# Both halves' delta rule in one software pipeline, and the samples' state update in two-head steps beside the output tiles

## The chip, the cores and the metric

The kernel runs on one core of a Trainium2 chip. The metric is the device time of one execution in microseconds; a kernel's time is the median of several executions.

## The reference, cut to what matters

The reference is one inference step of a two-layer decoder trunk for a prompt of 2048 tokens and 8 single-token samples, width 1024, all in float32. The change lies in the second (odd) layer:

```python
h = rmsnorm(x, norm_w)
q, k, v, u_sg, v_sg, b, a, gate = split(h @ w_in)      # 768, 768, 768, 256, 256, 6, 6, 1024 columns
q, k, v = split(silu(causal_conv4(concat(q, k, v))))   # 2304 channels
q = l2norm(q) * 128 ** -0.5 ; k = l2norm(k)            # 6 heads of 128
beta = sigmoid(b) ; logg = -exp(a_log) * softplus(a + dt_bias)
c_out = rmsnorm(gated_delta_rule(q, k, v, beta, logg, state))   # per token: S = exp(logg) S + k (beta (v - S'k))'
d_out = gelu(u_sg) * chunk_spatial_gate(rmsnorm(gelu(v_sg)))    # 128-token chunks, lower triangular
y = x + (concat(c_out, d_out) * silu(gate)) @ w_out
```

Outputs are `y` for prompt and samples, the new convolution rows and the new matrix states `S` (128 x 128 per head) of the prompt and of each of the 8 samples (`new_delta_sample`, 8 x 6 x 128 x 128).

## The kernel before, in words

**Matrix products.** Float32 products are made from two parts of each factor (`hi`, `lo`), three matmuls per product (`mm3`, L201 to L203). `fm_block` makes 128 output channels for a block of tokens (24 matmuls). Each 512 KB weight unit is loaded into the tile `wraw` (one buffer in this layer: `self.wbufs[2]` is 1), split by ScalarE (`whi`, L177) and VectorE or GpSimd (`wlo`, L179).

**Halves.** The prompt goes through the layer in two halves of 1024 tokens. For each half `odd` runs: 18 channel blocks `conv_silu` (three pieces of 342 or 340 tokens each; blocks 0 to 5 are q, 6 to 11 k, 12 to 17 v; the result goes to DRAM, `y1`); before block number `CB` = 14 the product for `v_sg`, `b`, `a` (`gated_v`, 8 or 9 token tiles) and the decays (`decay`); then `spatial` (6 pieces) and 24 gate pieces (`gate_block`, 8 units of three). After both halves come 17 output tiles (`out_tile`), the first four of them in two column halves. The output weights are loaded and split beside the first of these (`w_out`, L889 to L892).

**The delta rule** of a half is 16 items: 8 chunks of 128 tokens times two groups of three heads. Its stages are `delta_load` (q, k and decays from DRAM), `delta_front` (transposes and k k', k q' products), `delta_blocks` (VectorE solves 16 x 16 blocks, L1422 and L1424, with two round trips through DRAM), `delta_merge16` (loads v, L1447) and `delta_merge` (the inverse in 32, 64 and 128 wide blocks), `delta_step` (the recurrence through `S`; v is transposed in L1521) and `delta_out`. `blocks`, `merge16` and `merge` work on a pair of items. The table `DORD` gives each stage a lag of 0 to 6 items.

**Side work.** `delta`, `sample_delta` and `w_out` are Python generators in `self.sides`. A call `self.tick(n, kind)` writes the next n pieces of one of them at that place of the program; the delta rule's pieces are written at a high priority (`PRIO`). The final order on each engine is set when the program is built, by a scheduler that weighs the written order, the priorities and its own estimate of durations. On the chip every engine runs its own queue in that order and waits at each instruction until its inputs are there. All DMAs are issued by the SP queue.

**Where the delta rule's pieces stand.** After each half's convolution `self.tick(10000)` finishes the generator of the half before, and a new one is made. The first half's pieces then stand in that half's spatial part and gates and in the second half's convolution, one after each piece (`self.pace` is 1); the second half's in its spatial part, its gates and the output tiles. Output tile t of the second half is written once `self.ndone` items are finished.

**The samples' state.** `sample_delta` runs beside the second half's spatial part and gates. Its first part normalizes the samples' q and k (`rstd` in L125 and L126 on GpSimd), a second part multiplies each of the 8 states with k and q (L1629), and a third updates the states in 16 steps of three heads: load the state (L1649) and a broadcast correction row (L1650, from the DRAM tile `sdd`), three ScalarE multiplications (L1660), three VectorE multiply-adds (L1661), store (L1662). Its buffers are tiles `hx` of the pool `hp` (three buffers, one of them held by the samples' small tiles).

Of the kernel before, what the change touches and what calls it, by code (L numbers as in the profile page):

```python
# [10 lines left out]
F32 = mybir.dt.float32  # L11
# [4 lines left out]
ALU = mybir.AluOpType  # L16
# [4 lines left out]
P = 128  # L21
D = 1024
NT = 2048
NS = 8
NH = 6
# [3 lines left out]
HALF = 1024  # L29
# [7 lines left out]


T0, T1, T2 = 4, 2, 3
VA, VB, CB = 2, 5, 14  # L40
VS, SA = "P", 2
TS = 12
PC = 1
# [20 lines left out]
class Net:  # L64
# [1027 lines left out]
    def odd(self):  # L1092
        nc, I, O = self.nc, self.I, self.O
        st = ExitStack()
        self.banks = dict(OD, h=OD["acc"])
        self.odd_consts(st)
        wk = self.pool(st, "wk", 2)
        hp = self.hp
        dr = self.dram
        self.sg1 = dr.tile([D, NT + NS], F32, name="sg1")  # L1100
        self.cat1 = dr.tile([D, NT + NS], F32, name="cat1")
        self.vd = dr.tile([NT, 256], F32, name="vd")
        self.y1 = dr.tile([2304, NT], F32, name="y1")
        W = I["w_in_o"]
        for half in range(2):
            subs = self.subs if half == 0 else self.load_half(hp, wk)
            self.wsplit = WC if half else WB

            gates = [(W[i], P) for i in range(20, 28)]
            if half == 0:  # L1110
                We = I["w_out_e"]
                mix = [(We[i * 512:i * 512 + 512, cb * 256:cb * 256 + 256].rearrange("(k p) c -> p k c", p=P), 256)
                       for cb in range(4) for i in range(2)]
                gates = [u for g in range(6) for u in (gates[g], mix[g])] + mix[6:] + gates[6:]
            self.nxt = nxt = self.stream([(W[i], P) for i in range(CB)] + [(I["w_vba"][i], 268) for i in range(2)]
                                         + [(W[i], P) for i in range(CB, 20)] + gates, 1)
            for cb in range(18):
                if cb == CB:
                    ba = self.gated_v(half, subs, wk, hp)
                    gt = self.decay(half, ba, wk)  # L1120
                self.conv_silu(half, cb, nxt(), wk)
            if half:
                nc.sync.dma_start(O["new_conv_prompt"].rearrange("(k p) j -> p k j", p=P), self.clast,
                                  allow_slow_non_contiguous=True)
            if half == 0:
                self.tick(10000, "values")
                self.svst.close()
                dl = self.pool(st, "dl", 1, side="right")
            self.tick(10000)
            self.sides["delta"] = self.delta(half, gt, dl)  # L1130
            if half == 1:
                self.sides["sample"] = self.sample_delta(wk, hp)
            self.spatial(half, subs, wk, hp)
            if half == 1:
                self.sample_sg(wk)
            else:
                self.sides["sample"] = self.sample_out(wk, hp)
                self.tick(1, "sample")
            for g in range(6):
                unit = nxt()  # L1140
                for sub in subs:
                    self.gate_block(wk, g, unit, sub)
                    self.tick(half * SA, "sample")
                self.tick(1 - half, "sample")
            self.tick(2 * (1 - half), "sample")
            units = [nxt(), nxt()]
            for sub in subs:
                for g in range(2):
                    self.gate_block(wk, 6 + g, units[g], sub)
                    self.tick(half, "sample")  # L1150
        self.tick(10000, "sample")
        tiles = [tuple(a[:, :, c0:c0 + w] for a in (self.hh, self.hl)) for c0, w in QSUB]
        self.sides["w_out"] = self.w_out(I["w_out_o"], tiles, lambda: hp.tile([P, 4 + HALF], F32, tag="hx", name="wraw"), W2)

        def get(nm):
            if nm in ("whi", "wlo"):
                return self.wp.tile([P, D], F32R, tag=nm, name=nm, bufs=2)
            if nm[0] == "m":
                return self.t512(wk, nm)
            return hp.tile([P, 4 + HALF], F32, tag="hx", name=nm)[:, :D]  # L1160

        def out(t, *grps):
            n, t0 = (P, t * P) if t < 16 else (NS, NT)
            dst = O["y_prompt"][t0:t0 + n] if t < 16 else O["y_sample"]
            self.out_tile(t0, n, self.cat1, self.sg1, get, self.x1[t0:t0 + n], dst, grps)

        self.tick(4, "w_out")
        for t in range(T0):
            out(t, 0)
            self.tick(T1)  # L1170
            self.tick(2, "w_out")
        self.tick(10000, "w_out")
        for t in (*range(TS), 16, *range(TS, 16)):

            while 8 <= t < 16 and self.ndone < 2 * (t - 7):
                self.tick()
            out(t, *((1,) if t < T0 else (0, 1)))
            self.tick(T1 if t < T0 else T2)
        self.tick(10000)
        for g in range(2):  # L1180
            nc.sync.dma_start(O["new_delta_prompt"][g * 3:g * 3 + 3].rearrange("h k v -> k h v"), self.S[g])
        st.close()
# [61 lines left out]
    def conv_silu(self, half, cb, unit, wk):  # L1244

        nc = self.nc
        w = (self.convw, self.convh)[half][:, cb, :]
        for a, n in CSUB:
# [4 lines left out]
            x = self.t512(wk, "cx")[:, :n]  # L1253
# [11 lines left out]
                nc.scalar.activation(th, x, AF.Tanh)  # L1265
                nc.vector.scalar_tensor_tensor(th, th, 1.0, x, ALU.add, ALU.mult)
            self.store(self.y1[cb * P:cb * P + P, half * HALF + a:half * HALF + a + n], th)
            self.tick(self.pace)
            self.tick(1 if a else 2, "values")

    def t512(self, pool, name):
# [23 lines left out]
        nc.sync.dma_start(gd.rearrange("t h i -> (t h) i"), gr)  # L1295
        return beta, nG, kd, gd

    def delta(self, half, gt, dl):

        self.ndone = 0  # L1300
        pairs = [dict(half=half, t=t) for t in range(8)]
        items = [dict(half=half, t=t, g=g, pair=pairs[t]) for t in range(8) for g in range(2)]
        stages = dict(load=self.delta_load, front=self.delta_front, blocks=self.delta_blocks, merge16=self.delta_merge16,
                      merge=self.delta_merge, step=self.delta_step, out=self.delta_out)
        for i in range(len(items) + 6):

            for j, lag in DORD:
                if 0 <= i - lag < len(items):
                    x = items[i - lag]
                    pair = j in ("blocks", "merge16", "merge")  # L1310
                    if not pair or x["g"]:
                        stages[j](x["pair"] if pair else x, gt, dl)
                        if j != "load":
                            yield

# [247 lines left out]
    def sample_delta(self, wk, hp):  # L1563

        nc, I, O = self.nc, self.I, self.O
# [12 lines left out]
        x, tp = f("sx", [P, 18, NS]), f("stp", [P, 18, NS])  # L1578
# [17 lines left out]
        q, k, v = (x[:, i * 6:i * 6 + 6, :].rearrange("p h b -> p (h b)") for i in range(3))  # L1596
# [7 lines left out]
        bb = f("sbb", [P, 2, 48])  # L1604
# [12 lines left out]
        sd = I["state_delta"]  # L1617
# [5 lines left out]
        nx = load(0)  # L1623
# [18 lines left out]
        nc.tensor.transpose(pd[:48, :], dlt, self.ident)  # L1642
        dr = f("sdr", [48, P])
        nc.vector.tensor_copy(dr, pd[:48, :])
        dd = self.dram.tile([NH, NS, P], F32, name="sdd")
        nc.sync.dma_start(dd.rearrange("h b v -> (h b) v"), dr)
        def load2(b, g):
            s = hp.tile([P, 4 + HALF], F32, tag="hx", name="s1")[:, :768].rearrange("p (h v) -> p h v", v=P)
            nc.sync.dma_start(s[:, :3], sd[0, b, g:g + 3].rearrange("h k v -> k h v"))  # L1649
            nc.sync.dma_start(s[:, 3:], dd[g:g + 3, b:b + 1, :].rearrange("h o v -> o h v").broadcast_to([P, 3, P]))  # L1650
            return s[:, :3], s[:, 3:], b, g

        steps = [(b, g) for b in range(NS) for g in (0, 3)]
        nx = load2(*steps.pop(0))
        while nx:
            (s, db, b, g), nx = nx, load2(*steps.pop(0)) if steps else None
            yield
            for h in range(3):
                j = (g + h) * NS + b
                nc.scalar.mul(s[:, h, :], s[:, h, :], bb[:, 1, j:j + 1])  # L1660
                nc.vector.scalar_tensor_tensor(s[:, h, :], db[:, h, :], k[:, j:j + 1], s[:, h, :], ALU.mult, ALU.add)  # L1661
            nc.sync.dma_start(O["new_delta_sample"][b, g:g + 3].rearrange("h k v -> k h v"), s)  # L1662

        nc.vector.tensor_tensor(qkp, o, o, ALU.mult)
        yield
        pr = self.bank("side", P)
        mm(pr[:, :48], self.ones, qkp, start=True, stop=True)
        nc.vector.tensor_scalar(qkp, pr[:, :48], 1.0 / P, None, ALU.mult)
# [1 line left out]
        nc.vector.tensor_tensor(o, o, qkp, ALU.mult)  # L1670
        nc.vector.tensor_scalar(o, o, self.onw, None, ALU.mult)
        nc.sync.dma_start(self.cat1[:768, NT:].rearrange("(h p) b -> p h b", p=P), o.rearrange("p (h b) -> p h b", b=NS))

    def sample_sg(self, wk):
        nc, I, O = self.nc, self.I, self.O
# [123 lines left out]
```

## Time and profile before

| | us |
|---|---|
| three executions, median (lowest to highest) | 3059.98 (3048.13 to 3065.13) |
| profiled execution, its own time | 3062.73 |
| its span, first to last instruction | 3060.6 |

| engine | busy us | share |
|---|---|---|
| TensorE (PE) | 2788.8 | 91% |
| its weight loads (PEld) | 2535.1 | 83% |
| VectorE (DVE) | 2087.6 | 68% |
| GpSimd (POOL) | 1654.7 | 54% |
| ScalarE (ACT) | 1375.1 | 45% |

Busy shares are averages over stages with different limits; the odd layer's second half is the part from about 2095 us on. `PEclk` is the granted TensorE clock as a share of full speed (2.4 GHz); the two levels are 1.0 and 0.5, so 0.86 over a stretch means that 28% of it ran at 1.2 GHz. An idle time is put down to the event that ended it.

### The profile page before, as it was taken

Reading aid. Unit: us, or ns where it says so; the run is one execution under the profiler, and the core shown is the slowest. Engines: PE = TensorE matmul, PEld = TensorE weight load, DVE = VectorE, ACT = ScalarE, POOL = GpSimd, SP = SyncE. Lnnn points to the kernel's source line nnn. Section 1 sums busy time; section 2 is a strip of 40 time slices with the busy share of each in tenths; the row PEclk is TensorE's granted clock in tenths of the full one; section 3 lists DMA queues with packets and bytes.
Section 4 is the critical chain, followed back from the end, with each engine's and each line's share of the span. In section 5 each row is a group of like instructions: output and inputs, shape, how many; then the busy total and the mean of one; then the engine's idle time right before and its main releaser. Section 6 shows DMA issues by size and latency. Waiting matters only on the chain. (4 is left out here: it accounts for less than half of the span.)

```text
span 3060.6 us, 57584 instructions
## 1 busy us (share of the span) xinstructions
PE 2788.8 (91%) x20425; PEld 2535.1 (83%) x20425; DVE 2087.6 (68%) x4067; ACT 1375.1 (45%) x3995; POOL 1654.7 (54%) x1249
## 2 busy tenths in 40 slices
PE   8998999999998899989888989999999879788999
PEld 8998999989777777769778878878899868677887
DVE  5465466563998899875677877568877574556652
ACT  5323332224877787762223233445554533444331
POOL 5666546550666876665675655454544253256541
PEclk9999999999999999999999999999999989989999
DMA  6779988868234413227776655444333234467543
GB/s 233 255 242 317 319 280 297 257 198 238 58 90 118 124 56 91 73 79 218 237 239 202 195 178 166 133 128 126 104 94 97 87 83 117 131 190 209 147 113 100
DMA packets 440154, 506.57 MB, mean 166 GB/s; under 512 B 86331, under 2 KB 339684, under 8 KB 439868
## 3 DMA queue, kind: packets, MB, share of 16 engines
q1 hardware_dynamic: 439868, 502.90, 54.0%
q8 instruction: 162, 2.65, 0.4%
q14 instruction: 124, 1.02, 0.1%
HBM read 347.09 MB, written 155.69 MB: 164 GB/s over the span
## 5 line engine op out<-in xcount | busy, mean ns | idle before, releaser
L201 PE MATMUL acc<-bh,whi 128*128 128x256 f32 (+4 forms) x1208 | 406.2, 336 | 15.9 <-ACT whi L910 6.7
L202 PE MATMUL acc<-bl,whi 128*128 128x256 f32 (+4 forms) x1208 | 404.4, 335 | 0.9 <-DVE bl L892 0.9
L203 PE MATMUL acc<-bh,wlo 128*128 128x256 f32 (+4 forms) x1208 | 402.6, 334 | 2.7 <-DVE wlo L911 1.8
L855 POOL TENSOR_TENSOR p<-p,cf 128x512 f32<-128x512 f32 (+3 forms) x240 | 236.8, 1005 | 218.6 <-DVE cf L839 69.8
L832 ACT ACTIVATE p<-sc,nb 128x512 f32<-128x512 f32 (+3 forms) x480 | 302.2, 642 | 73.4 <-DVE nb L831 59.8
L645 POOL TENSOR_TENSOR kp<-kp,at 128x768 f32<-128x768 f32 x120 | 201.4, 1687 | 173.2 <-DMA kp<-in_cache_v 152.2
L203 PE MATMUL cv<-bh,wlo 128*128 128x346 f32 (+2 forms) x864 | 284.3, 330 | 6.4 <-DVE wlo L179 4.4
L831 DVE TENSOR_REDUCE nb<-sc 128x1 f32<-128x512 f32 (+3 forms) x480 | 276.1, 598 | 18.7 <-PE sc L830 9.4
L201 PE MATMUL cv<-bh,whi 128*128 128x346 f32 (+2 forms) x864 | 284.8, 330 | 2.9 <-DVE vv L1036 1.8
L202 PE MATMUL cv<-bl,whi 128*128 128x346 f32 (+2 forms) x864 | 284.5, 329 | 0.0
L567 POOL TENSOR_TENSOR kp<-kp,qb 128x768 f32<-128x768 f32 x88 | 166.2, 1894 | 191.0 <-DMA kp<-in_cache_k 145.2
L201 PEld LDWEIGHTS acc<-bh,whi 128*128 128x128 f32 (+1 forms) x1208 | 232.7, 193 | 32.6 <-ACT whi L910 7.6
L201 PE MATMUL acc<-whi,bh 128*128 128x256 f32 x864 | 247.8, 287 | 7.6 <-ACT whi L177 6.0
L202 PE MATMUL acc<-wlo,bh 128*128 128x256 f32 x864 | 247.1, 286 | 2.7 <-POOL wlo L179 1.9
L203 PEld LDWEIGHTS acc<-bh,wlo 128*128 128x128 f32 (+1 forms) x1208 | 232.4, 192 | 19.5 <-DVE wlo L911 2.9
L203 PE MATMUL acc<-whi,bl 128*128 128x256 f32 x864 | 246.5, 286 | 0.0
L202 PEld LDWEIGHTS acc<-bl,whi 128*128 128x128 f32 (+1 forms) x1208 | 232.6, 193 | 15.2 <-DVE bl L892 1.3
L647 DVE TENSOR_TENSOR sacc<-sacc,kp 128x768 f32<-128x768 f32 x120 | 184.2, 1535 | 78.7 <-POOL kp L645 68.6
L827 PE MATMUL sc<-kh,q 128*128 128x512 f32 (+2 forms) x480 | 210.5, 439 | 25.3 <-ACT p L832 22.0
L869 PE MATMUL pv<-v,pt 128*128 128x128 f32 x1632 | 219.1, 282 | 15.2 <-ACT pt L867 8.5
L869 PEld LDWEIGHTS pv<-v,pt 128*128 128x128 f32 x1632 | 202.6, 195 | 29.8 <-ACT junk L872 13.6
L179 POOL TENSOR_TENSOR wlo<-wraw,whi 128x1024 fp32r<-128x1024 f32 (+1 forms) x62 | 151.7, 2449 | 89.2 <-ACT whi L177 77.7
(445 smaller groups left out, 8339.8 us busy)
## 6 DMA issues: line engine op xcount, KB each, us to landing
kp<-in_cache_k SPq DMA_DIRECT2D x128, 384.0 KB
kp<-in_cache_v SPq DMA_DIRECT2D x128, 384.0 KB
wraw<-in_w_in_o SPq DMA_DIRECT2D x56, 512.0 KB
mc<-cat SPq DMA_DIRECT2D x72, 256.0 KB
mg<-sg SPq DMA_DIRECT2D x72, 256.0 KB
wraw<-in_w_in_e SPq DMA_DIRECT2D x28, 512.0 KB
wsplit<-whi SPq DMA_DIRECT2D x28, 512.0 KB
wsplit<-wlo SPq DMA_DIRECT2D x28, 512.0 KB
```

The lines of the kernel that those rows point to most:

```text
L179: e.tensor_tensor(lo, raw, hi.bitcast(F32), ALU.subtract)
L201: mm(out, ah, bh, start=first, stop=False)
L202: mm(out, ah, bl, start=False, stop=False)
L203: mm(out, al, bh, start=False, stop=last)
L567: (nc.vector if j % 3 == 2 else nc.gpsimd).tensor_tensor(k, k, qb, ALU.mult)
L645: nc.gpsimd.tensor_tensor(h3(w), h3(v), self.at[:, b, j, :, None].broadcast_to([P, NH, P]), ALU.mult)
L647: nc.vector.tensor_tensor(acc, acc, v, ALU.add)
L827: mm(sc[:, :w], qc, kh[:, c, :w], start=True, stop=False)
L831: nc.vector.tensor_reduce(nb[:, c, j:j + 1], sc[:, :n], AX.X, ALU.max, negate=True)
L832: nc.scalar.activation(p[:, c, :n], sc[:, :n], AF.Exp, bias=nb[:, c, j:j + 1], accum_out=l[:, c, j:j + 1])
L855: nc.gpsimd.tensor_tensor(p[:, 1, :n], p[:, 1, :n], cf[:, 1, j:j + 1].broadcast_to([P, n]), ALU.mult)
L869: mm(pv, tt[:, t, :], kvt[j][2][:, t, :], start=j == 0 and t == 0, stop=j * 4 + t == nk - 1)
```

## The change

The two delta generators become one over 32 items. Items of the second half may load q and k once `self.ready` is 1 (from channel block 12 on), and load v and go into `merge16` once it is 2 (after the second half's convolution); until then the generator gives its turn away. The first half's pieces are no longer finished by `tick(10000)`. In the second half `gated_v` and `decay` move from before channel block 14 to before block 10, and a convolution block gets two pieces of the delta rule, not three. The samples' state update leaves `sample_delta`; it becomes a generator of its own, `sample_state`, with 24 steps of two heads, whose two buffers lie in one tile of `wraw`. It is written from the output weights on, one or two steps per output tile. Two small tiles (`skg`) keep the samples' k and decay for it.

```diff
-VA, VB, CB = 2, 5, 14
+VA, VB, CB = 2, 5, (14, 10)
@@ odd
+        self.ndone, self.gts, self.ready = 0, [], 0
         for half in range(2):
...
             for cb in range(18):
-                if cb == CB:
+                if cb == CB[half]:
                     ba = self.gated_v(half, subs, wk, hp)
-                    gt = self.decay(half, ba, wk)
+                    self.gts.append(self.decay(half, ba, wk))
+                if half and cb == 12:
+                    self.ready = 1
                 self.conv_silu(half, cb, nxt(), wk)
...
-                dl = self.pool(st, "dl", 1, side="right")
-            self.tick(10000)
-            self.sides["delta"] = self.delta(half, gt, dl)
+                self.sides["delta"] = self.delta(self.pool(st, "dl", 1, side="right"))
+            else:
+                self.ready = 2
             if half == 1:
+                self.sdd = dr.tile([NH, NS, P], F32, name="sdd")
+                self.skg = wk.tile([P, 2, NH * NS], F32, name="skg", bufs=1)
                 self.sides["sample"] = self.sample_delta(wk, hp)
...
         self.tick(10000, "sample")
+        self.sides["state"] = self.sample_state()
...
         for t in range(T0):
             out(t, 0)
             self.tick(T1)
+            self.tick(1, "state")
             self.tick(2, "w_out")
...
-            while 8 <= t < 16 and self.ndone < 2 * (t - 7):
+            while 8 <= t < 16 and self.ndone < 2 * (t + 1):
                 self.tick()
             out(t, *((1,) if t < T0 else (0, 1)))
             self.tick(T1 if t < T0 else T2)
+            self.tick(1 if t < T0 else 2, "state")
         self.tick(10000)
+        self.tick(10000, "state")
@@ conv_silu
-            self.tick(self.pace)
+            self.tick(self.pace if a else 0)
@@ delta
-        self.ndone = 0
-        pairs = [dict(half=half, t=t) for t in range(8)]
-        items = [dict(half=half, t=t, g=g, pair=pairs[t]) for t in range(8) for g in range(2)]
+        pairs = [dict(half=half, t=t) for half in range(2) for t in range(8)]
+        items = [dict(half=y["half"], t=y["t"], g=g, pair=y) for y in pairs for g in range(2)]
...
-                        stages[j](x["pair"] if pair else x, gt, dl)
+                        while x["half"] and self.ready < dict(load=1, merge16=2).get(j, 0):
+                            yield
+                        stages[j](x["pair"] if pair else x, self.gts[x["half"]], dl)
@@ sample_delta
...
+        nc.sync.dma_start(self.sdd.rearrange("h b v -> (h b) v"), dr)
+        nc.vector.tensor_copy(self.skg[:, 0, :], k)
+        nc.vector.tensor_copy(self.skg[:, 1, :], bb[:, 1, :])
+    def sample_state(self):
+        nc, sd, out = self.nc, self.I["state_delta"], self.O["new_delta_sample"]
+        buf = self.wp.tile([P, 2, 2, 2, P], F32, tag="wraw", name="sbuf", bufs=self.wbufs[2])
+
+        def load(i):
+            b, g = i // 3, i % 3 * 2
+            s = buf[:, i % 2]
+            nc.sync.dma_start(s[:, 0], sd[0, b, g:g + 2].rearrange("h k v -> k h v"))
+            nc.sync.dma_start(s[:, 1], self.sdd[g:g + 2, b:b + 1, :].rearrange("h o v -> o h v").broadcast_to([P, 2, P]))
+
+        n = 3 * NS
+        load(0)
+        for i in range(n):
+            if i + 1 < n:
+                load(i + 1)
+            yield
+            b, g = i // 3, i % 3 * 2
+            s = buf[:, i % 2]
+            for h in range(2):
+                j = (g + h) * NS + b
+                nc.scalar.mul(s[:, 0, h, :], s[:, 0, h, :], self.skg[:, 1, j:j + 1])
+                nc.vector.scalar_tensor_tensor(s[:, 0, h, :], s[:, 1, h, :], self.skg[:, 0, j:j + 1], s[:, 0, h, :], ALU.mult, ALU.add)
+            nc.sync.dma_start(out[b, g:g + 2].rearrange("h k v -> k h v"), s[:, 0])
```

The changed kernel's line numbers are 10 to 22 higher in these functions (L1521 becomes L1533, L1661 becomes L1693, L1447 becomes L1459). Three places show how the built order moves.

TensorE, in the second half's last convolution blocks, where v of the second half's first item is transposed (`rr<-ident,v`; `cv` is a convolution piece, `fr` the delta rule's front). Before, it stands in the second piece of block 15:

```order
L203 MATMUL cv_29935<-bh,wlo 128x346
L201 MATMUL cv_29969<-bh,whi 128x346
L202 MATMUL cv_29969<-bl,whi 128x346
L203 MATMUL cv_29969<-bh,wlo 128x346
L1368 MATMUL fr<-ident,qk 128x128 x3
L1521 MATMUL rr<-ident,v 128x128 x3
```

Now it stands in the last piece of block 16:

```order
L201 MATMUL fr<-qh 128x256
L202 MATMUL fr<-cm,qh 128x256
L203 MATMUL fr<-qh,cm 128x256
L1533 MATMUL rr<-ident,v 128x128 x3
L203 MATMUL cv_30172<-bh,wlo 128x352
L201 MATMUL cv_30226<-bh,whi 128x346
```

The transposes need the results of blocks 12 to 14. Before, one piece stood between the last of these and them; now nearly six do. In all, 14,878 TensorE instructions stood ahead of the second half's first spatial product (L1225, now L1235), and 14,980 stand there now; the whole list has 18,025 in both kernels.

VectorE, in the second half's gates, the state's multiply-adds (L1661, now L1693; `th` is a gate piece, `vt`, `re`, `ks` are the delta rule's). Before, in the middle of the gates:

```order
L1661 SCALAR_TENSOR_TENSOR s_31606<-s_31606,arena 128x128 x3
L1522 TENSOR_TENSOR vt<-rr,ks 128x384
L439 SCALAR_TENSOR_TENSOR th<-th,acc 128x512
L1661 SCALAR_TENSOR_TENSOR s_31705<-s_31705,arena 128x128
L1422 TENSOR_TENSOR ut<-nn,uu 48x15
```

Now the first of them stand at the sixth piece from the last:

```order
L1437 COPY uu<-uu 48x256
L1693 SCALAR_TENSOR_TENSOR sbuf<-sbuf,skg 128x128 x2
L1542 TENSOR_TENSOR re<-vt,rr 128x384
L1693 SCALAR_TENSOR_TENSOR sbuf<-sbuf,skg 128x128 x2
L439 SCALAR_TENSOR_TENSOR th<-th,acc 128x512
L1407 TENSOR_SCALAR ks<-kss 128x6
L1693 SCALAR_TENSOR_TENSOR sbuf<-sbuf,skg 128x128 x4
L439 SCALAR_TENSOR_TENSOR th<-th,acc 128x512
```

Of the 48 multiply-adds, 22 (11 steps) stand among the last six gate pieces and 26 (13 steps) behind them, the last ahead of the result of the ninth half-tile of the output; before, all 48 stood among the last twelve gate pieces.

SP, at the beginning of the output tiles (`mc`, `mg`, `ox` are an output tile's inputs, `wraw` the output weights). Before:

```order
L905 DMA ox<-x_17772 128x512
L902 DMA mg<-sg_20429 128x4x128
L902 DMA mc<-cat_20430 128x4x128
L902 DMA mg<-sg_20429 128x4x128
L1560 DMA cat_20430<-o 128x3x128
L555 DMA out_y_prompt<-ox 128x512
L889 DMA wraw<-in_w_out_o 128x2x256 x2
```

Now:

```order
L1679 DMA sbuf<-in_state_delta 128x2x128
L1459 DMA v<-y_20432 128x3x128
L1680 DMA sbuf<-sdd 128x2x128
L889 DMA wraw<-in_w_out_o 128x2x512
L1694 DMA out_new_delta_sample<-sbuf 128x2x128
L1680 DMA sbuf<-sdd 128x2x128
L1344 DMA gb<-grow_28949 128x384
L905 DMA ox<-x_17772 128x512
L902 DMA mc<-cat_20430 128x4x128
```

Each of 13 steps puts two loads and a store between those of the tiles and of the delta rule.

## Rows read from the trace of the kernel before

**Rows 1.** Page: busy time and instructions of each engine; clock in 40 slices.

```profile
PE 2788.8 (91%) x20425; PEld 2535.1 (83%) x20425; DVE 2087.6 (68%) x4067; ACT 1375.1 (45%) x3995; POOL 1654.7 (54%) x1249
PEclk9999999999999999999999999999999989989999
```

**Rows 2.** Windows: stretch, length, busy per engine (count), PEclk, DMA share, GB/s.

```profile
2095.00:2425.00 330.00, 321.14 (x2748) 303.80 (x2746) 256.90 (x634) 174.37 (x553) 145.55 (x111) 1.00 0.34 98
2425.00:2475.00 50.00, 40.77 (x262) 40.34 (x263) 28.92 (x65) 23.98 (x71) 16.84 (x11) 0.86 0.28 92
2475.00:2550.00 75.00, 57.27 (x416) 48.72 (x415) 44.02 (x101) 20.44 (x60) 41.95 (x25) 0.82 0.34 68
2550.00:2612.00 62.00, 61.60 (x530) 56.09 (x530) 27.68 (x86) 23.08 (x74) 19.64 (x17) 1.00 0.45 131
2612.00:2712.00 100.00, 74.50 (x494) 65.76 (x487) 47.90 (x139) 37.98 (x140) 37.58 (x25) 0.88 0.56 147
2712.00:2840.00 128.00, 111.07 (x894) 97.10 (x895) 88.03 (x181) 59.24 (x190) 73.25 (x58) 0.92 0.74 211
2840.00:3035.00 195.00, 190.52 (x1595) 167.05 (x1590) 99.77 (x240) 62.41 (x231) 76.40 (x64) 0.99 0.43 121
```

**Rows 3.** Waits of PE, 2425 to 2475: line, ended by, us, times, longest.

```profile
PE rr L1521 <- DMA v<-y: 10.1, 1, 10.1
```

**Rows 4.** Waits of PE, 2475 to 2550.

```profile
PE side L1613 <- DVE arena L1610: 10.7, 1, 10.7
PE acc L201 <- DVE dd L1230: 3.7, 1, 3.7
PE acc L1225 <- DVE ga L1036: 1.7, 2, 1.4
PE side L1589 <- DVE A L1380: 1.5, 1, 1.5
```

**Rows 5.** Timeline of GpSimd and of SP around those two waits: start, us, instruction.

```profile
2498.73 15.66 POOL L126 TENSOR_TENSOR arena<-arena,mhalf 128x96 f32<-128x96 f32 x1
...
2417.88 0.30 SPq L1603 DMA_DIRECT2D sbgd<-arena  x1
...
2427.36 0.33 SPq L1605 DMA_DIRECT2D arena<-sbgd  x1
...
2430.61 0.37 SPq L1447 DMA_DIRECT2D v<-y  x1
```

**Rows 6.** Waits in 2612 to 2712 of ACT, DVE, SP and PE, the longest.

```profile
ACT s L1660 <- DMA s<-in_state_delta: 39.9, 10, 7.1
DVE s L1661 <- DMA s<-sdd: 40.1, 12, 6.3
SPq L1649 <- DMA out_new_delta_sample<-s: 13.1, 9, 3.9
PE fr L201 <- DVE A L1380: 6.5, 1, 6.5
```

**Rows 7.** Tile `s`: duration ns min/median/max, first and last start us.

```profile
L1660 ACT ACTIVATE s<-s,arena x48: 385/389/411, 2602.9 to 2702.8; 128x128 f32<-128x128 f32 x48
L1661 DVE SCALAR_TENSOR_TENSOR s<-s,arena x48: 336/347/2143, 2617.4 to 2705.5; 128x128 f32<-128x128 f32 x48
```

**Rows 8.** Timeline of one state step and its neighbour: SP, then DVE, then PE.

```profile
2658.59 1.34 SPq L1650 DMA_DIRECT2D s<-sdd  x1
...
2664.93 0.37 SPq L1649 DMA_DIRECT2D s<-in_state_delta  x1
2665.35 0.48 SPq L1650 DMA_DIRECT2D s<-sdd  x1
...
2664.46 2.14 DVE L1661 SCALAR_TENSOR_TENSOR s<-s,arena 128x128 f32<-128x128 f32 x1 [3.49 <-DMA s<-sdd]
...
2667.82 0.54 DVE L1535 TENSOR_TENSOR re<-rr,kc 128x384 f32<-128x384 f32 x1
...
2670.30 1.36 DVE L1661 SCALAR_TENSOR_TENSOR s<-s,arena 128x128 f32<-128x128 f32 x2 [0.31 <-DMA s<-sdd]
...
2668.41 0.49 PE L1539 MATMUL do<-re,A 128*128 128x128 f32 x2 [2.76 <-DVE re L1535]
```

More of the change, by code (lines that the diff above doesn't have):

```diff
@@ L1114, in odd @@
                 gates = [u for g in range(6) for u in (gates[g], mix[g])] + mix[6:] + gates[6:]
-            self.nxt = nxt = self.stream([(W[i], P) for i in range(CB)] + [(I["w_vba"][i], 268) for i in range(2)]
-                                         + [(W[i], P) for i in range(CB, 20)] + gates, 1)
+            self.nxt = nxt = self.stream([(W[i], P) for i in range(CB[half])] + [(I["w_vba"][i], 268) for i in range(2)]
+                                         + [(W[i], P) for i in range(CB[half], 20)] + gates, 1)
             for cb in range(18):
-                if cb == CB:
+                if cb == CB[half]:
                     ba = self.gated_v(half, subs, wk, hp)
-                    gt = self.decay(half, ba, wk)
+                    self.gts.append(self.decay(half, ba, wk))
+                if half and cb == 12:
+                    self.ready = 1
                 self.conv_silu(half, cb, nxt(), wk)
@@ L1296, in decay, with delta @@
         return beta, nG, kd, gd
-    def delta(self, half, gt, dl):
-        self.ndone = 0
-        pairs = [dict(half=half, t=t) for t in range(8)]
-        items = [dict(half=half, t=t, g=g, pair=pairs[t]) for t in range(8) for g in range(2)]
+    def delta(self, dl):
+        pairs = [dict(half=half, t=t) for half in range(2) for t in range(8)]
+        items = [dict(half=y["half"], t=y["t"], g=g, pair=y) for y in pairs for g in range(2)]
         stages = dict(load=self.delta_load, front=self.delta_front, blocks=self.delta_blocks, merge16=self.delta_merge16,
@@ L1644, in sample_delta @@
         nc.vector.tensor_copy(dr, pd[:48, :])
[L1645 to L1662, printed above, removed]
+        nc.sync.dma_start(self.sdd.rearrange("h b v -> (h b) v"), dr)
+        nc.vector.tensor_copy(self.skg[:, 0, :], k)
+        nc.vector.tensor_copy(self.skg[:, 1, :], bb[:, 1, :])
+        yield
         nc.vector.tensor_tensor(qkp, o, o, ALU.mult)
-        yield
         pr = self.bank("side", P)
@@ L1672, in sample_delta @@
         nc.sync.dma_start(self.cat1[:768, NT:].rearrange("(h p) b -> p h b", p=P), o.rearrange("p (h b) -> p h b", b=NS))
+    def sample_state(self):
[11 more added lines that the diff above has]
+                load(i + 1)
+            yield
+            b, g = i // 3, i % 3 * 2
[5 more added lines that the diff above has]
+            nc.sync.dma_start(out[b, g:g + 2].rearrange("h k v -> k h v"), s[:, 0])
     def sample_sg(self, wk):
```

## The prediction

> **What bounds the kernel now.** I read the page first, then the windows, then the waits of the stretches in which TensorE is not full. The page shows TensorE busy for 91% of the span and no other engine above 68% [rows 1], so time is to be found where TensorE stands still or runs at the low clock. The windows show where, in the part that the change touches [rows 2]. While the first half's delta rule runs beside the second half's convolution (2095 to 2425 us), TensorE is idle for 330.00 - 321.14 = 8.9 us, 2.7%, at full clock. From 2425 to 2550 us the delta rule's first half is finished and its second has barely begun: idle 9.2 + 17.7 = 27.0 us, and a granted clock of 0.86 and 0.82 takes up to 0.14 x 50 + 0.18 x 75 = 20.5 us more. From 2550 to 2612, gates beside the delta rule, 0.4 us is idle. From 2612 to 2712, where the samples' state is updated, 25.5 us, and up to 12 for the clock. From 2712 to 2840 (output weights and first half-tiles) 16.9 us, and up to 10. From 2840 to 3035 TensorE is busy for 190.5 of 195: full.
>
> The waits name the causes. Before 2475 one wait of 10.1 us is all: the transposes of v for the second half's first item [rows 3]. SP issues that load at 2430.6; until 2427.4 it stood behind a tiny round trip of the samples' decays, issued at 2417.9 [rows 5]. In the spatial part the longest wait (10.7) ends with the samples' normalized q and k, and before it GpSimd spends 15.66 us on one power of 128 x 96 elements [rows 4, 5]. From 2612 on ScalarE waits 39.9 and VectorE 40.1 us for the state's loads [rows 6], and because queues are in order the delta rule behind them waits too: VectorE stands 3.49 us before a state row, the delta rule's `re` comes at 2667.8, and TensorE stands 2.76 us for it [rows 8].
>
> **The change part by part.** The sum is made against the profiled execution, 3062.7 us (span 3060.6 and 2.1 around it), which is 2.7 above the median of the three.
>
> *A. One pipeline (2425 to 2550).* The built order moves 102 delta instructions of TensorE ahead of the spatial part; the number of instructions stays, so this work costs nothing where it goes but fills gaps. The wait for v: nearly six convolution pieces now stand between the last result it needs and the transposes, against one before. The first stretch holds 15 blocks of three convolution pieces and the 9 of `gated_v`, 54 in 330 us, 6.1 us each [rows 2], so the load has some 30 us more: 10.1 us go, and about 3 of the low clock that follows. The three short waits of the spatial part (3.7 + 1.7 + 1.5 = 6.9) are for evictions with nothing else to do; delta steps of two items now stand there, and I take half, 3.5. The clock in that stretch costs up to 13.5; I take 5, since the longest wait stays: the power on GpSimd is not touched, and the work between the two samples' products is no longer than before. Something is late next: the second item's v is transposed right behind the first spatial piece, with one piece between it and the convolution, and SP's stop for the decays now falls earlier, before other stores. The first such wait cost 10.1; I put 0 to 8 on it and take 3. Sum of A: 10.1 + 3 + 3.5 + 5 - 3 = 18.6 us gained. Ends: 2 (only the first wait goes, and 8 come back) and 47 (all idle and low clock of the stretch).
>
> *B. The state in the gates (2612 to 2712).* The stretch before it, with the same gates and delta rule, idles 0.4 us, so nearly all 25.5 us could be the state's; the delta rule's own chain has 2.7% elsewhere, and I take 20 for the state and 4 of the clock's 12: 24 us for 16 steps, 1.5 each. Now 11 steps stand there, each with two thirds of the bytes. If the hold scales with bytes a step costs 1.0, if not 1.5; I take the middle, 1.25. Left: 11 x 1.25 = 13.8, so 10 gained. Ends: 0 (the chain's own waits were the cause) and 25.5 - 11 x 1.0 = 14.
>
> *C. The state beside the output tiles (2712 to 2840).* Thirteen steps come, each with two ScalarE operations of 0.389 and two VectorE ones of 0.347 us [rows 7]: 10 and 9 us, on engines busy for 59 and 88 of 128. They cost little by themselves; what counts is the holding of the queues. At 1.25 a step it is 16 us. But a step has 128 / 13 = 9.8 us here against (2705.5 - 2617.4) / 16 = 5.5 before [rows 7], and a correction row issued at 2665.4 was used at 2670.3, 4.9 us later [rows 8], so half of the steps should find their data there: 8 us lost. SP's queue matters too: a state load waited 13.1 us in 9 cases for the store before it [rows 6], and now mc, mg and the output weights stand behind such loads. Ends: 0, and 16 + 24 = 40: the steps bring 13 x 3 x 131 KB = 5.1 MB, and at this stretch's 211 GB/s that is 24 us if its transfers already set its pace.
>
> A rule of the Trainium skill speaks against the smaller steps: "DMA: Bandwidth & Descriptors", section "Anatomy of one DMA", gives a DMA a fixed cost of about 2 us that does not shrink with its size (measured there for GpSimd's DMAs). Of the 4.9 us here two thirds would then be 2 + 2.9 x 2/3 = 3.9 and not 3.3; with a hold of 1.2 to 1.3 a step the sum stays within 2 us of mine.
>
> *D. The rest.* From 2840 on TensorE is full, and the built order is nearly the same from the tenth pair on; whatever is won before is kept, and nothing is added: 0. Spreading the first half's pieces (two a block, not three) over blocks that had none moves work within a stretch that idles 2.7%: 0, with 3 either way. The two copies into `skg` are small VectorE operations once: nothing.
>
> Sum: 18.6 + 10 - 8 = 20.6 us gained, 3062.7 - 20.6 = 3042.1; less the 2.7 by which the profiled execution lies above the median, 3039.4. I predict **3040 us**.
>
> **The rivals.**
>
> *The gap moves.* The built orders meet again at the tenth pair's merge, where both have the same steps and fronts done: what was put into the gap is missing in the gates behind it. If the power and the second v hold the spatial part as before, and the state's holds in the gates go down only with the number of steps, A gives 5, B 7 (5 of 16 steps of 1.5), C costs 8: 3058.7 for the profiled run, 3056 as a median. For it: the 10.7 us wait is untouched, and GpSimd's 15.66 us now also stand before delta operations. Against it: the 10.1 us wait has a cause that goes.
>
> *Everything fills.* A gives 40, because steps of two items keep TensorE and its clock up during GpSimd's power, B 14, C costs 4: 50 gained, 3010 as a median. For it: with the delta rule beside the convolution only 2.7% were idle. Against: the order is fixed at build time, and an in-order queue stops at the first late input.
>
> *The output tiles become the bound (slower).* The stretch of 2712 to 2840 has the highest DMA share of all, 0.74 [rows 2], and SP feeds it from one queue. If its transfers set its pace, C costs 24 for the bytes and 16 for the holds; with 10 from A and 8 from B that is 22 lost: 3082. It decides from the point at which that stretch (to the eighth half-tile) is more than 29 us longer than before, the gains of A and B together. Against it: 0.74 is not 1, and 128 us at full share would carry 211 / 0.74 x 128 = 36.5 MB where 27.0 + 5.1 are wanted.
>
> **How the numbers follow.** Forecast 0.42, the gap moves 0.22, everything fills 0.22, slower 0.14. The range takes the forecast's own ends and reaches to the second and third cases and into the fourth: 3006 to 3074. This kernel's measurement tells about 0.5%, 15 us, from no change. The forecast lies 20 under the median: two thirds of its chance fall beyond 15 us (0.28), one third within (0.14). Faster: 0.28 + 0.22 + 0.05 of the moved gap = 0.55; within: 0.14 + 0.17 + 0.01 = 0.32; slower: 0.13.
>
> **What would show it.** A: no wait for v of some 10 us in the last convolution blocks; the time from the second half's first convolution piece to the first gate 10 to 25 us shorter; the 10.7 us wait for the samples' second product still there. B: TensorE's idle time over the second half's 24 gates down by about 10 us, ScalarE's and VectorE's waits for state loads present only in the last six pieces. C: those waits at about half of the 13 steps between the first output tiles, and that stretch some 8 us longer. D: TensorE over 95% busy from the ninth half-tile to the last item. I am wrong if the spatial part idles as before, or if the output tiles' loads wait for SP behind state loads.

## The result, and the profile after

The changed kernel takes 3032.78 us (median of five, 3026.53 to 3037.70) against 3059.98 before: a ratio of 0.9918, 95% interval 0.9897 to 0.9939, so 25 us (19 to 32) faster. A second set of six on another chip gave 0.9928 (0.9908 to 0.9948). The profiled execution took 3031.84 us, 30.9 less than that of before. On its page TensorE is as busy as before, in a shorter span [rows 1]:

```profile
PE 2781.6 (92%) x20425; PEld 2530.5 (84%) x20425; DVE 2084.7 (69%) x4069; ACT 1370.6 (45%) x3995; POOL 1657.5 (55%) x1249
```

To compare stages I cut both traces at the same events of the program: the second half's first convolution eviction, its first and its last gate eviction, the eighth half-tile of the output, and the last output; the cuts are at whole us, up to 2 us beside the event. Windows of before between these (columns as in [rows 2]: length, then busy time of PE, PEld, DVE, ACT, POOL, the clock, DMA share, GB/s):

```profile
2099.00:2537.00 438.00, 402.18 (x3240) 377.11 (x3238) 319.14 (x776) 207.97 (x654) 196.04 (x142) 0.95 0.33 92
2537.00:2715.00 178.00, 152.10 (x1201) 136.61 (x1201) 84.22 (x242) 69.63 (x240) 61.91 (x43) 0.93 0.50 135
2715.00:2822.00 107.00, 90.47 (x686) 78.73 (x685) 77.98 (x159) 53.40 (x176) 60.68 (x48) 0.90 0.75 214
2822.00:3056.00 234.00, 226.03 (x1864) 198.51 (x1862) 111.44 (x265) 67.72 (x243) 91.70 (x77) 0.98 0.44 124
```

The same four of after:

```profile
2095.00:2540.00 445.00, 413.33 (x3423) 386.32 (x3423) 338.93 (x835) 215.70 (x692) 207.19 (x151) 0.97 0.35 94
2540.00:2691.00 151.00, 139.54 (x1079) 126.36 (x1077) 61.34 (x157) 54.40 (x186) 50.49 (x33) 0.93 0.39 112
2691.00:2793.00 102.00, 85.97 (x625) 74.96 (x626) 79.73 (x184) 55.73 (x182) 62.18 (x47) 0.93 0.94 271
2793.00:3025.00 232.00, 224.32 (x1855) 198.07 (x1854) 114.86 (x266) 68.70 (x247) 90.16 (x76) 0.98 0.45 129
```

Convolution and spatial part take 7 us longer, with 183 more TensorE instructions in them; the gates take 27 less, the first half-tiles 5 less, the rest 2 less. TensorE's idle time (length less busy) goes from 35.8, 25.9, 16.5 and 8.0 us to 31.7, 11.5, 16.0 and 7.7.

Waits of TensorE in after, 2095 to 2420, then 2420 to 2540 (what waits, what ended it, us, times, longest). The wait for v [rows 3] is gone. A new one of 5.8 has come, and the samples' wait, 10.7 in [rows 4], is 12.2; of the three short spatial waits, 6.9 us, one of 0.7 is left, and another of 0.7 has come:

```profile
PE cv L201 <- DVE cx L1266: 5.8, 1, 5.8
...
PE side L1625 <- DVE arena L1622: 12.2, 1, 12.2
PE acc L1235 <- DVE dd L1240: 0.7, 1, 0.7
PE side L1709 <- DVE arena L1626: 0.7, 1, 0.7
```

The state's waits, which were 39.9 us on ScalarE alone [rows 6]: ScalarE and SP in 2650 to 2691 (the first begins at 2647), then ScalarE in 2691 to 2810, where the last steps lie.

```profile
ACT sbuf L1692 <- DMA sbuf<-in_state_delta: 26.0, 10, 4.6
SPq L1679 <- DMA out_new_delta_sample<-sbuf: 3.3, 4, 1.5
...
ACT sbuf L1692 <- DMA sbuf<-in_state_delta: 12.4, 7, 5.1
```

In the last gates, with 11 steps, ScalarE stands for 26 of the 44 us from 2647 to 2691. From there to 2810 it stands 12.4: 1.3 for the eleventh step and 11.1 in six of the 13 that lie beside the output tiles.

### The profile page after: what moved, and what is told of

It reads as the page before. It is cut to its first block, busy times and chain, and to the rows that moved or that the text cites. A ratio compares the mean times of both kernels' runs of the same rounds, so it can differ in the third digit from the quotient of the medians.

```text
span 3030.1 us, 57607 instructions
## 1 busy us (share of the span) xinstructions
PE 2781.6 (92%) x20425; PEld 2530.5 (84%) x20425; DVE 2084.7 (69%) x4069; ACT 1370.6 (45%) x3995; POOL 1657.5 (55%) x1249
## 5 line engine op out<-in xcount | busy, mean ns | idle before, releaser
L647 DVE TENSOR_TENSOR sacc<-sacc,kp 128x768 f32<-128x768 f32 x120 | 176.2, 1469 | 81.5 <-POOL kp L645 71.1
```

Source lines behind the costliest of these rows:

```text
L647: nc.vector.tensor_tensor(acc, acc, v, ALU.add)
```

## The experiments

All were run several times beside the kernel before, four to a chip. The ratio is that to before; an interval is about 0.002, 6 us, to either side, so differences of 5 us between two of them are told by the trace and not by the time. The next four columns are the lengths of the four stretches above, each between its own events in one profiled execution, and the last is their sum.

| kernel | median us | before beside it | ratio (interval) | conv. to gate | gates | half-tiles | rest | sum |
|---|---|---|---|---|---|---|---|---|
| before | | | | 438 | 178 | 107 | 234 | 957 |
| changed | 3032.78 | 3059.98 | 0.9918 (0.9897 to 0.9939) | 445 | 151 | 102 | 232 | 930 |
| state_only | 3048.01 | 3055.76 | 0.9977 (0.9963 to 0.9990) | 438 | 165 | 106 | 240 | 949 |
| pipe_only | 3047.25 | 3055.76 | 0.9972 (0.9957 to 0.9986) | 442 | 164 | 107 | 232 | 945 |
| after_no_state | 3015.63 | 3055.76 | 0.9865 (0.9846 to 0.9884) | 444 | 138 | 105 | 231 | 918 |
| before_no_state | 3022.65 | 3055.76 | 0.9899 (0.9883 to 0.9914) | 437 | 151 | 102 | 230 | 920 |
| no_copy | 3024.15 | 3056.62 | 0.9899 (0.9877 to 0.9922) | 440 | 147 | 104 | 234 | 925 |
| no_trip | 3031.13 | 3056.62 | 0.9921 (0.9898 to 0.9944) | 436 | 150 | 102 | 236 | 924 |
| short_power | 3023.93 | 3056.62 | 0.9906 (0.9882 to 0.9930) | 436 | 149 | 103 | 234 | 922 |
| late | 3047.01 | 3056.62 | 0.9963 (0.9946 to 0.9980) | 444 | 138 | 111 | 250 | 943 |
| after_gates | 3028.08 | 3058.67 | 0.9901 (0.9884 to 0.9919) | 447 | 138 | 100 | 239 | 924 |
| two_waits | 3022.66 | 3058.67 | 0.9885 (0.9867 to 0.9902) | 427 | 148 | 108 | 238 | 921 |
| all | 3024.22 | 3058.67 | 0.9882 (0.9865 to 0.9900) | 426 | 141 | 105 | 253 | 925 |
| changed again | 3036.58 | 3058.67 | 0.9928 (0.9908 to 0.9948) | 443 | 148 | 104 | 236 | 931 |

The changed kernel was profiled twice, and its stretches differ by up to 4 us between the two. These executions came to the second half's first convolution eviction at 2095 and 2101 us, and over all kernels that event lies between 2090 and 2109. Even in before (2099) and before_no_state (2090), which are written alike up to there, it differs. So what lies ahead of the change moves the time of an execution too; the sums leave it out.

### The two parts apart: state_only, pipe_only

The first is before with `sample_state` and its ticks, `CB` and `delta` as they were; the second is after with the state loop of before back in `sample_delta`:

```diff
-        self.sides["state"] = self.sample_state()
...
-            self.tick(1 if t < T0 else 2, "state")
```

> The kernel before with the state update alone moved (24 steps of two heads in the weights' raw buffer); each half keeps its own delta generator. Theory (both parts win apart, the state's part in the gates): of the 31 us between the two profiled executions 14 are TensorE idle time of the 24 gates, and they go with the state steps, so this kernel takes 12 to 16 us less than before, 3044 to 3048, with the gates' idle time near 12 and the drained stretch still with its 10 us wait for v. Rival (the gates got better because delta work had left them for the convolution): within 4 us of before, 3056 to 3064, gates' idle time above 20.

> The changed kernel with the state update put back as it was (16 steps of three heads in sample_delta). Theory: the pipeline alone wins the rest, 11 to 15 us, 3045 to 3049; its gates idle by 20 or more, and no wait for v. Rival (the pipeline does it all): 3031 to 3037. Second rival (the pipeline only moves the gap from the convolution into the gates): 3056 to 3064.

Gates of state_only and of pipe_only:

```profile
2537.00:2702.00 165.00, 150.18 (x1264) 135.77 (x1261) 80.61 (x219) 66.76 (x234) 64.49 (x45) 0.95 0.42 117
...
2540.00:2704.00 164.00, 139.26 (x1010) 126.07 (x1009) 65.71 (x184) 57.95 (x195) 46.73 (x31) 0.91 0.49 136
```

In the gates the parts add up: the state's move takes 13 us off (178 to 165, and 164 to 151 on top of the pipeline), the pipeline 14 (178 to 164, 165 to 151), and it pays 4 to 7 of them before the gates. None of the rivals holds. In time they win 7.0 (3 to 11) and 8.5 (4 to 13) us, 15.5 in sum, against 25 and 22 for both; by the sums of the stretches 8 and 12, against 27 and 26. The theory wanted 11 to 16 each, and state_only's gates idled 14.8, not near 12. One TensorE wait in state_only's last stretch (240 us), for which its trace gives no cause, may be part of the missing 6 to 10 us (its row in 2808 to 3048):

```profile
PE fr L1367 <- issue: 6.2, 1, 6.2
```

Whether the parts really help each other stays open: the intervals allow it and allow none.

### The price of the state: after_no_state, before_no_state

```diff
-        n = 3 * NS
+        n = 3
```

and in before `range(NS)` to `range(1)` in the list of steps.

> The changed kernel with 3 of the 24 state steps left (the states of samples 1 to 7 are not updated). Theory: the 11 steps in the last gates still cost most of the 10 us of idle time and 3 of clock there, and those beside the first half-tiles, at a DMA share of 0.94, about half of that stretch's 16 idle us: 15 to 22 us less than the changed kernel, 3011 to 3018. Rival (the steps are hidden now, the idle time there belongs to the delta rule and the output weights): 3028 to 3033.

> The kernel before with 2 of the 16 state steps left (the states of samples 1 to 7 are not updated). The prediction put 24 us on the 16 steps: 3037 to 3041 by that. Rival (the delta rule's own chain makes the gates idle): 3052 to 3060.

Gates and first half-tiles of after_no_state, then of before_no_state:

```profile
2538.00:2676.00 138.00, 133.84 (x1078) 121.40 (x1077) 57.17 (x149) 50.45 (x179) 50.10 (x32) 0.96 0.35 102
2676.00:2781.00 105.00, 85.75 (x619) 73.05 (x617) 83.08 (x153) 48.92 (x152) 68.02 (x51) 0.95 0.77 222
...
2527.00:2678.00 151.00, 146.85 (x1275) 133.10 (x1274) 76.47 (x206) 62.84 (x224) 64.99 (x47) 0.99 0.38 107
2678.00:2780.00 102.00, 87.02 (x684) 75.81 (x683) 81.01 (x164) 49.35 (x155) 69.54 (x54) 0.97 0.81 235
```

In before the 14 steps cost 33 us by the medians, 27 of them in the gates, more than the 24 put on all 16; the rival (the delta rule's own chain) falls. The trace of before shows how. Its longest TensorE wait there is 6.5 us, for the delta rule's `A` (L1380) [rows 6]; on VectorE that operation stood behind two state steps that waited for their correction rows:

```profile
2627.82 0.88 DVE L1661 SCALAR_TENSOR_TENSOR s<-s,arena 128x128 f32<-128x128 f32 x3 [5.41 <-DMA s<-sdd]
2632.15 0.35 DVE L1661 SCALAR_TENSOR_TENSOR s<-s,arena 128x128 f32<-128x128 f32 x1 [3.46 <-DMA s<-sdd]
2633.27 0.42 DVE L1380 TENSOR_TENSOR A<-fr,A 128x256 f32<-128x256 f32 x1
```

In before_no_state TensorE's longest wait in the gates is 1.6 us.

In after 21 steps cost 16 us (0.9918 to 0.9865), as the theory had it in size but not in place: 13 in the gates, where 8 of them lay (the three that are left stand there too), and nothing beside the half-tiles, which take 105 us without the steps and 102 with them, though their DMA share goes from 0.77 to 0.94.

### The new wait of 5.8 us: no_copy, no_trip

SP and VectorE in after, around that wait (start, us, instruction):

```profile
2345.63 0.30 SPq L1615 DMA_DIRECT2D sbgd<-arena  x1
...
2354.95 0.33 SPq L1617 DMA_DIRECT2D arena<-sbgd  x1
...
2361.20 0.38 SPq L1344 DMA_DIRECT2D gb<-grow  x1
...
2358.39 0.19 DVE L1659 COPY skg<-arena 128x48 f32<-128x48 f32 x1 [8.95 <-DMA arena<-sbgd]
2358.49 0.57 DVE L1266 SCALAR_TENSOR_TENSOR cx<-cv,convh,cx 128x342 f32<-128x342 f32 x1
```

The copy into `skg`, one of the two new VectorE operations, waits for the samples' decays, and the convolution's evictions stand behind it. The decays make a round trip of 0.4 KB through DRAM; the store is issued at 2345.63, the load only 9.3 us later, and SP issues nothing else in the last 7.5 of these. no_copy takes the copy away, no_trip the round trip:

```diff
-        bb = f("sbb", [P, 2, 48])
+        bb = self.skg[:, 1:3, :]
...
-        nc.vector.tensor_copy(self.skg[:, 1, :], bb[:, 1, :])
```

```diff
-        nc.sync.dma_start(bd.rearrange("s h b -> b s h"), bg, allow_slow_non_contiguous=True)
-        nc.sync.dma_start(bb, bd.rearrange("s h b -> (s h b)")[None, :].broadcast_to([P, 96]))
...
+        nc.vector.tensor_tensor(b8, bg.rearrange("p s h -> p (s h)")[:, :, None].broadcast_to([NS, 12, NS]),
+                                self.ident[:NS, None, :NS].broadcast_to([NS, 12, NS]), ALU.mult)
...
+        mm(pb[:, :96], self.ones[:NS], bb[:NS].rearrange("p s j -> p (s j)"), start=True, stop=True)
...
```

> The changed kernel, with the samples' decays broadcast by their DMA straight into a lasting tile, so that the copy skg<-arena (L1659), before which VectorE stood 8.95 us, is gone. Theory SP (what costs is SP's stop for the round trip, and every load behind it is late whatever VectorE does): another wait of 4 to 6 us takes the place of the 5.8 at the convolution, within 4 us of the changed kernel, 3029 to 3035; the row that shows it is a TensorE wait behind the decays' row gb, as in the pipeline-only kernel (5.2 us there). Rival (the copy alone is the cause): the wait of 5.8 us goes and the half clock behind it: 6 to 9 us less, 3024 to 3027.

> The changed kernel with the samples' decays spread over the partitions by one product with ones (128 x 96) in place of the round trip through DRAM: SP's stop of 8 us is gone, the copy into skg stays. Theory SP: both waits go, no TensorE wait over 2 us between 2095 and 2420, clock 1.00 there, 6 to 9 us less than the changed kernel: 3024 to 3027. Rival (the tiny transfer is hidden): 3031 to 3035.

The longest TensorE wait in 2095 to 2420 and VectorE's behind it in no_copy, then the longest of TensorE in no_trip:

```profile
PE oo L1569 <- DVE o L1561: 4.8, 2, 4.5
...
DVE el L1368 <- ACT gb L1366: 4.5, 1, 4.5
...
PE dm L1465 <- POOL T L1456: 3.0, 5, 1.3
```

The rows decide for SP: without the copy the delta rule's row `gb`, issued behind the stop, is late and TensorE waits 4.5 us for it; without the round trip neither wait is left, and the stretch is 436 us. The times do not follow: no_copy fell where its rival wanted it, no_trip was no faster than the changed kernel. Both intervals reach over the other's median, so the value of this cut is not settled by the times. By the sums of the stretches both are 5 to 7 us below the changed kernel (925 and 924, against 930 and 931).

### The samples' power: short_power

```diff
-        mm(pn[:, :96], self.ones, tp[:, :12, :].rearrange("p k b -> p (k b)"), start=True, stop=True)
...
-        self.rstd(rn, 4 * EPS)
...
+        mm(pn[:96, :1], tp[:, :12, :].rearrange("p k b -> p (k b)"), self.ones[:, :1], start=True, stop=True)
...
+        self.rstd(r1[:96], 4 * EPS)
...
+        nc.vector.tensor_scalar(rn[:96], self.ident[:96, :96], r1[:96], None, ALU.mult)
...
+        mm(pn[:, :96], self.ones[:96], rn[:96], start=True, stop=True)
```

> The changed kernel with the samples' norms summed on 96 partitions, so that GpSimd's power works on 96 x 1 elements, not 128 x 96, and the result is spread by a second product with ones. Theory: the 12.2 us wait for the samples' normalized q and k goes, and most of the half clock around it (0.83 in 2490 to 2540, 8 us): 12 to 18 us less than the changed kernel, 3015 to 3021. Rival (the rest of that chain, two products and three VectorE steps in an in-order queue, is as long): a wait of 4 to 8 us stays, 3026 to 3030.

GpSimd's power in after and in short_power, and the longest wait of TensorE in 2420 to 2545 of the latter:

```profile
2501.52 15.66 POOL L126 TENSOR_TENSOR arena<-arena,mhalf 128x96 f32<-128x96 f32 x1
...
2497.28 0.57 POOL L126 TENSOR_TENSOR arena<-arena,mhalf 96x1 f32<-96x1 f32 x1
...
PE side L1608 <- DVE arena L1606: 3.1, 1, 3.1
```

The wait falls from 12.2 to 3.1 us, the stretch from 445 to 436. The time, 0.9906, lies between theory and rival.

### The state later: late, after_gates

The written place of the steps does not set their order: in the changed kernel they are written behind the gates, and 11 of the 24 stand among the last six gate pieces all the same. So late takes its buffers from the ring of the output tiles and writes the steps later, and after_gates writes one column of each buffer from the last gate piece first (in both an excerpt):

```diff
-            s = buf[:, i % 2]
+            s = self.t512(self.odwk, "sbuf").rearrange("p (x h v) -> p x h v", x=2, v=P)
...
```

```diff
+        for i in range(2):
+            nc.gpsimd.tensor_copy(buf[:, i, 0, 0, :1], self.last[:, :1])
...
```

> The changed kernel with the state's buffers taken from the ring of 128 x 512 tiles that the output tiles use, and written one step for each of the first tiles and two for each later one, so that no step stands in the gates and the 24 steps lie between the fourth and the last output tile. Theory (steps cost where they crowd TensorE's own work and nothing where they have 7 us and more each): the gates lose the 13 us that lie between 151 and the 138 us of the kernel almost without steps, and the output stretch stays: 8 to 13 us less than the changed kernel, 3020 to 3025. Rival (the ring is now too short: output tiles wait for their tiles behind state stores): 3033 to 3050.

> The changed kernel with the state's two buffers kept in the weights' raw tile, but written once from the last gate piece before the first load, so that no step can stand in the gates: 24 steps between the first output tile and the thirteenth. Theory (a step is dear in the gates, where SP's queue and the next weights stand behind it, and free beside the output tiles as long as it takes no tile from them): gates 138 us as in the kernel almost without steps, first half-tiles within 4 us of 102, 8 to 13 us less than the changed kernel. Rival (24 steps at 7 us each fill SP's queue, at a DMA share of 0.94 already): the first half-tiles take 8 to 15 us longer and eat it, within 4 us of the changed kernel or slower.

The last three stretches of late, then of after_gates:

```profile
2540.00:2678.00 138.00, 133.73 (x1078) 121.91 (x1077) 55.24 (x141) 48.94 (x172) 50.25 (x33) 0.96 0.32 94
2678.00:2789.00 111.00, 95.30 (x699) 83.29 (x698) 83.38 (x177) 53.09 (x167) 66.46 (x52) 0.91 0.80 233
2789.00:3039.00 250.00, 223.44 (x1784) 196.21 (x1782) 116.04 (x290) 75.99 (x274) 82.80 (x70) 0.96 0.51 142
...
2544.00:2682.00 138.00, 133.91 (x1080) 122.00 (x1079) 54.46 (x144) 49.11 (x173) 50.01 (x32) 0.96 0.33 96
2682.00:2782.00 100.00, 83.21 (x622) 72.59 (x621) 80.97 (x175) 53.00 (x170) 62.70 (x50) 0.95 0.90 259
2782.00:3021.00 239.00, 227.78 (x1855) 200.05 (x1854) 127.61 (x290) 75.94 (x270) 89.83 (x75) 0.97 0.52 147
```

Both bring the gates to 138 us with no step there, which is also the length with the three steps of after_no_state: the 11 steps of the changed kernel cost 13 us together, the first three of them nothing that shows. late gives back 9 and 18 us in the next two stretches, as its rival said, and SP shows the ring as a cause (waits in 2678 to 3039):

```profile
SPq L902 <- DMA out_new_delta_sample<-sbuf: 11.6, 10, 2.8
```

Ten times an output tile's input (L902) waited for a state step's store to free its tile; after_gates, with as many steps there and buffers of its own, has no such wait. How much of the 27 us is the ring is not shown, since late's steps also run later (2729 to 2951 us, against 2696 to 2847). after_gates takes 100 us for the half-tiles, gives back 3 to 7 in the last stretch (239, against 236 and 232), and is 8.5 us faster than the changed kernel on the same chip, at the lower end of the theory; the two intervals overlap a little.

### Together: two_waits, all, and the changed kernel again

two_waits has the edits of no_trip and short_power, all has those and that of after_gates; the changed kernel ran beside them.

> The changed kernel with both of the spatial part's chains cut: the decays spread by a product, and the power on 96 x 1 elements. By the stage times of the two kernels that cut one each (436 us from the second half's first convolution piece to its first gate in both, against 445), 15 to 20 us go in that stretch. Theory (nothing gives it back): 14 to 20 us less than the changed kernel. Rival (the delta rule's chain takes half back in the gates and the last tiles, as in those two kernels, which from the first gate on took 488 and 486 us against 485): 6 to 12 us less.

> Both together: the decays by a product, the short power, and the state steps behind the gates. Theory: the sum, 22 to 33 us less than the changed kernel, 3000 to 3010. Rival (one of them takes the other's place, since the gates wait for the delta rule once the state is gone): no more than the better of the two, 3012 to 3020.

> The changed kernel once more, unchanged, on the chip of the three others, as their base: 3026 to 3038 by its first five runs; all theories the same.

The first stretch and, in what follows, one late wait of two_waits (in 2700 to 3040):

```profile
2103.00:2530.00 427.00, 411.89 (x3437) 384.65 (x3436) 336.80 (x840) 216.04 (x695) 193.18 (x153) 0.99 0.37 99
...
PE acc L201 <- ACT whi L910: 10.5, 2, 9.8
```

Cutting both chains takes 16 us off the stretch (443 to 427), and two_waits is 13.9 us faster than the changed kernel beside it, just short of the theory's 14 to 20; from the first gate on it took 494 us against 488. all is no faster than two_waits: its rival, though at 3024 and not 3012 to 3020. Its gates are 141 us, but its last stretch took 253, so that the four sum to 925, against 921 for two_waits. That execution took 3040 us, 16 above the kernel's median, but it came to its first convolution eviction only at 2109 us; how much of the 16 lies in the last stretch, and what its other runs have there, is not known. two_waits and all are 1.15% and 1.18% faster than before, and both faster than the changed kernel on the same chip (0.72%).

## Why the prediction was right, and where its steps were not

The forecast was 3040 us (3006 to 3074) and the time 3033, faster with a chance of 0.55. But that the sum came so near is in part luck: A was put some 10 us too high, B and C some 4 and 8 too low.

*A, 18.6 us: the mechanism held, the size and the place did not.* The wait for v went, the three short waits fell from 6.9 to 0.7, and the clock rose from 0.95 to 0.97, worth (0.05 x 438) - (0.03 x 445) = 9 us where 8 were put. But idle time fell only 4.1 where 10.1 + 3.5 - 3 was put: the new wait is 5.8, not 3, and it is not for the second item's v but behind SP's stop, which the prediction had named and put in the wrong place; the power's wait grew by 1.5, and the rest went in small waits. The first sign of being wrong was half there: over the last 64 us before the first gate TensorE idles 14.0 us, at a clock of 0.87, against 17.7 at 0.79 before. The prediction wrote "The two copies into `skg` are small VectorE operations once: nothing": they last 0.19 and 1.28 us, but the shorter one is the first VectorE instruction to need the round trip. Alone the pipeline is worth 8.5 us (4 to 13), nearer to the 5 that the first rival put on A than to 18.6. And the sign shown was wrong: the stretch from convolution to gates became 7 us longer, not 10 to 25 shorter. The step of A that failed is "this work costs nothing where it goes but fills gaps": TensorE is 11.2 us busier in that stretch (402.2 to 413.3) and idle only 4.1 less. Moved work lengthens the stretch that takes it and shortens the one that it leaves, here by 14 us in the gates.

*B, 10 us: mechanism and place held.* The steps' price was put at 24 us before and 13.8 after; the runs give 27 in the gates for 14 of the 16 steps, and 13 for the 11 that stand there now, so 14 won where 10 was put (13 where the state moved alone). In the gates ScalarE's waits for state loads begin only at 2647 us, with the first step. What one step costs does not come out cleanly: 27 us are 1.9 for each of the 14 steps taken away, or 1.7 if the two left are free; 13 us are 1.2 for each of 11, or 1.6 for each of the 8 whose removal was enough. The Trainium skill's fixed cost of about 2 us a DMA ("DMA: Bandwidth & Descriptors", "Anatomy of one DMA"; given for GpSimd's DMAs, where these are SP's) would make two heads cost more than two thirds of three. The prices above put that ratio anywhere from 0.6 to nearly 1, so no run here decides it.

*C, a loss of 8: wrong.* The half-tiles became 5 us shorter, and the runs without steps took 105 us against 102. ScalarE did wait in six of the 13 steps, near the half that was said, 11.1 us, but TensorE lost nothing that shows. That no input that TensorE needed next stood behind these holds is the likely reason; no run shows it. SP did stand at state loads with the tiles' loads behind them, the second sign of being wrong, but only 4.8 us in three cases (2691 to 2810). The slower rival built on the same stretch: its share rose to 0.94, as its bytes wanted, and still it set no pace.

*D, 0: right.* TensorE is busy for 224.32 of 232 us there, 97%, and 2 us were won.

So about 8.5 + 14 + 0 by these runs where 18.6 + 10 - 8 was written. The terms are not of one kind: 8.5 is a difference of medians and 14 a length in single executions. By the ratios alone, the state's move (B and C, written as 2) is worth 7.0 us on the kernel before and 16.5 on top of the pipeline (0.9972 to 0.9918), so how the 25 us divide stays open.

## What to carry to other kernels

Price a new instruction by what it waits for and by what stands behind it on its queue, not by its duration. When work moves between stretches, compare the sum of both, and expect the gain where the work has left. A step that holds an in-order queue can be dear in one stage (here 13 us for 11 steps in the gates) and free in the next (13 steps beside the first output tiles). In a kernel whose order a scheduler sets, such a step is moved by a dependency or by the buffer it takes, and the place where it is written may not move it.

## What the runs showed of the hardware

GpSimd's power took 15.66 us for 128 x 96 elements in the changed kernel, and 8.03 for 128 x 48, 0.86 for 128 x 3 and 0.57 for 96 x 1 in short_power: it goes with the elements of one partition. A round trip of 0.4 KB through DRAM in the changed kernel held SP until 9.3 us after its store, and its data was used 3.4 us later. The first half-tiles had a DMA share of 0.77 (222 GB/s) in after_no_state and 0.94 (271 GB/s) in the changed kernel, and were not longer with it (105 and 102 us).
